# A streaming conformer layer on one core: rows loaded at the fourth gate, taps pinned behind score minima, the channel mean later, a12 moved in odd gates, outputs stored by ScalarE

## The chip, the cores and the metric

One core of a Trainium2 chip runs the whole program. The metric is the time of one execution in microseconds on the device: the kernel before took 3021.13 us in the median of three runs (3019.73 to 3027.58).

Five engines work side by side, each in the order of its own instruction stream: TensorE (PE; its weight loads are listed apart as PEld), VectorE (DVE), ScalarE (ACT), GpSimd (POOL) and SyncE (SP, which here only issues DMAs). An instruction that waits for another engine holds up everything behind it on its own engine. L103 is the line of a helper that records every compute operation, so nearly all compute rows of the profile carry it, and rows are told apart by their tiles.

## What is computed

2048 prompt tokens and 64 sample tokens of width 1024 go through one layer: normalise, one input projection, a convolution branch and a chunk-band attention branch, a gated merge with an output projection, and a gated feed-forward network. Cut to what matters:

```python
h = rms_norm(x, norm1_g) * (1 + sc1) + sh1
glu_a, glu_b, q, k, v, g_conv, g_attn = split(h @ w_in)      # 512 512 512 512 512 1024 1024
u = glu_a * sigmoid(glu_b)
y = depthwise_conv(concat(hist, u), w_dw) + b_dw             # 31 taps, causal, 512 channels
conv_out = silu(layer_norm(y)) @ w_conv_out                  # mean and variance over channels
s = q_h . k_h / 8 + rel_bias; mask to the 64-token chunk and the 8 chunks before it
attn_out = softmax(s) @ v_h @ w_attn_out                     # 8 heads of 64, q and k normed
x = x + gt1 * ((sigmoid(g_conv) * conv_out + sigmoid(g_attn) * attn_out) @ w_o)
gate, up = split((rms_norm(x, norm2_g) * (1 + sc2) + sh2) @ w_ffn_in)   # 2816 each
y_out = x + gt2 * ((silu(gate) * up) @ w_ffn_out)
```

Outputs are y for prompt and sample, and the last convolution inputs, keys and values as states.

## The kernel before

**Number format.** Products of fp32 values are made from high and low halves: an operand is `hi` (rounded, a ScalarE copy) and `lo` (the rest, a subtraction on VectorE or GpSimd), and three matmuls, hi by hi, hi by lo, lo by hi, make one product (`mm3`). In the rows `whi` and `wlo` are halves of weights, `hh` and `hl` of the normalised x, `ph` and `pl` of probabilities.

**Phase 1** runs over four token blocks: 0 to 576 (with the 64 sample tokens), then three of 512. Each block goes through the stages q, 0, k, 1, v, 2, 3, g. The stages q, k and v are projections with rows out. The stages 0 to 3 make u for 128 channels each (`glu`), and start `convolve`: one multiply and thirty multiply-adds on VectorE, one per further tap (rows y<-u,wd,y; 128x606 elements in block 0, else 128x512), into a tile y that has a single buffer. Stage g makes 16 tiles of gates, numbered from 0.

**Work beside the stages** runs in lanes: generators that are pumped between TensorE's products by a planner. The planner adds up estimated load for each engine (`stream.load["pe"]` is its clock, in ns of TensorE) and lets a generator go on when its due time (`yield <time>`) is reached. The order in which this emits instructions is, with a few exceptions, the order on each engine; no times of a real run enter it. The lanes are the norm tiles of the next block, attention heads, the convolution's taps, and the tail.

- *Attention heads.* Block b's heads start after its stage v, so they run beside stages 2, 3 and g and the next block's first stages. A head makes scores tile by tile (rows sc<-kk,q; four matmuls of 128x320 for a full tile) in a PSUM tile with one buffer. VectorE adds the bias and takes the minimum of the negated scores (`softmax_max`; a row named ISA in the order and CUSTOM_DVE_ANT_0 in the trace, pr<-sc,bias), which frees the tile for the next scores; then come exponentials, transposes (ptp) and the product with v (po).
- *Norm tiles* (`norm_tile`). Four tiles of 128 tokens belong to the next block. Each loads its rows x (`load_x`, 512 KB, three buffers, shared with v's stores `vst`), squares on ScalarE, takes the root on GpSimd and VectorE, scales x, makes two groups of four transposes (pt<-ident,x_t), scales them on VectorE, copies hh on ScalarE and subtracts hl on VectorE. The lane is filled at gate 11 (`NORM_G`) and two tiles run at once; a tile that is not done when its first product is due is drained.
- *The tail* (`conv_norm`). When a block's taps are done, GpSimd adds the channels, TensorE makes the mean (pm<-s,ones), VectorE subtracts it, squares are added, a second pm gives the variance, and root, reciprocals, tanh and scales give the branch's silu. At the next block's stage 0 taps and tail are drained.

**Phase 2** runs over three column passes (0 to 576, 576 to 1344, 1344 to 2112). Each merges the two branches with the gates (tg, loaded again from memory), multiplies by w_o, normalises, and runs the feed-forward network over 22 gate tiles f. Gate and up products of a tile are made on 2x2 blocks with seven products instead of eight, named s2, s3, s1, a12, a22, a11 and s4; a product of one half (288 columns in the first pass, 384 in the others) is four times three matmuls. In `up`, s1 accumulates into the PSUM bank that s2 began and that ScalarE has copied to u2 (tile u); a12 has a bank of its own, with a sum and a silu behind it. From f = 5 (`EARLY`) on a12 is made in this way and a11 is made a gate ahead. `up_operands` lists the same order for the producer of the operands; `dn_at` lists the places (`at(n)`) inside an odd gate at which pieces of the down product of a pair are put. The last down product adds into acc, and its rows are stored by SP (L2067) at a due time behind VectorE.

Of the kernel before, what the change touches and what calls it, by code (L numbers as in the profile page):

```python
# [44 lines left out]
TURN_LAG = 2500.0  # L45
KN_LAG = 5000.0
X_LAG = 8000.0
ON_POOL = ()
DMA_LAG = 4000.0
OUT_LAG = 4000.0  # L50
# [2 lines left out]
SIDE_G = 10  # L53
SPLIT_G = 2
NORM_G = 11
NORM_W = 2
SCORE_ROOM = {"dve": 2500}
TURN_NS = 600.0
# [481 lines left out]
def up_operands(f):  # L540

    ops = (["s2", "s3", "s1"] if f else ["s3", "s2", "s1"]) + ["a12"] * (f >= EARLY) + ["a22"] + ["a11"] * (EARLY <= f + 1 < NF) + ["s4"]
    return [(f + (op == "a11"), op) for op in ops]


def dn_at(f):

    return (0, 1, 3, 6 if f == PAIRS[-1] else 4)  # L550


def mod_order():
# [34 lines left out]
def streaming_layer(ctx: ExitStack, tc: tile.TileContext, I, O):  # L588
# [512 lines left out]
    def square(x_t, n):  # L1101
# [4 lines left out]
        dve.tensor_tensor(ssq[:n, 0:1], ssq[:n, 0:1], ssq[:n, 1:2], ALU.add)  # L1106
        return rsqrt_mean(wk, ssq[:n, 0:1], n, 1, D)

    def norm_tile(lo, t, free):

        c = slice(t - lo, t - lo + P)
        x_t = load_x(t, P, wa, "x", 3)
        yield stream.load["pe"] + X_LAG
        r = square(x_t, P)
        yield stream.when("pool")
        dve.tensor_scalar(x_t, x_t, r, None, ALU.mult)
        yield stream.when("dve") + PE_LAG
        for g in range(2):
            pt = ps_g.tile([P, 4, P], F32, tag="gp", name="pt")
            h = temp("h32", (P, 4, P))  # L1120
            for k in range(4):
                pe.transpose(pt[:, k], x_t[:, (4 * g + k) * P : (4 * g + k + 1) * P], ident)
            stream.after("dve", "pe")
            for k in range(4):
                kk = 4 * g + k
                dve.tensor_scalar(h[:, k], pt[:, k], A1[:, kk, 0:1], B1[:, kk, 0:1], ALU.mult, ALU.add)
            yield stream.when("dve")
            yield lambda: free["columns"] >= c.stop
            f = slice(4 * g, 4 * g + 4)
            act.activation(hh[:, f, c], h, AF.Copy)  # L1130
            yield stream.when("act")
            dve.tensor_tensor(hl[:, f, c], h, hh[:, f, c].bitcast(F32), ALU.subtract)
# [66 lines left out]

    now = {"scored": -1, "finished": -1, "bias": None}  # L1200

    def convolve(u, y, ct, b):
        w = UW if b == 0 else HIST + QB
        n = w - HIST
        states = [(cs_s, HIST + SMP)] if b == 0 else [(cs_p, w)] if b == len(PBLOCKS) - 1 else []
        if states:
            yield stream.when("dve") + TURN_LAG
        for rows_, e in states:
            pt = ps_g.tile([P, 512], F32, tag="gp", name="pt")
            pe.transpose(pt[:HIST, :P], u[:, e - HIST : e], ident)  # L1210
            s = wa.tile([HIST, P], F32, tag="cc", name="cc", bufs=2)
            dve.tensor_scalar(s, pt[:HIST, :P], 0.5, None, ALU.mult)
            stream.at(stream.when("dve"), lambda s=s, rows_=rows_: nc.sync.dma_start(rows_[:, ct * P : (ct + 1) * P], s))
            yield
        gps.tensor_copy(hist[:, ct], u[:, w - HIST : w])
        dve.tensor_scalar(y[:, ct, :n], u[:, :n], wd[:, ct, 0:1], bdw[:, ct : ct + 1], ALU.mult, ALU.add)
        for k in range(1, TAPS):
            dve.scalar_tensor_tensor(y[:, ct, :n], u[:, k : k + n], wd[:, ct, k : k + 1], y[:, ct, :n], ALU.mult, ALU.add)
            yield

    def conv_norm(y, c0, n, t0):
        yv = y[:, :, c0 : c0 + n]
        yield lambda: not conv.gens
        s = wk.tile([P, 512], F32, tag="ln_s", bufs=1)

        def total():
# [311 lines left out]
    for b, stage in ORDER:  # L1538
        lo, hi = PBLOCKS[b]
        if stage == "q":  # L1540
            free, ahead = {"columns": 0}, {}
            if b + 1 < len(PBLOCKS):
                ahead = {t: norm_tile(hi, t, free) for t, _ in token_tiles(*PBLOCKS[b + 1])}
        if stage == "q" and b == 0:
            pass
        elif stage in ("q", "k", "v"):
            qkv(b, "qkv".index(stage), norms)
            if stage == "v":

                def heads(b=b):  # L1550
                    work.drain()
                    stream.flush()
                    attention(b)
                    if b == 3:
                        attn.burst, attn.spacing = 2, 0.0

                stream.at(stream.load["pe"] + HEADS_NS, heads)
        elif stage == "g":
            for g in gates(b, free):
                if g == NORM_G:  # L1560
                    for gen in ahead.values():
                        norm_lane.add(gen)
                if g == SIDE_G and b == len(PBLOCKS) - 1:
                    work.drain()
                    conv.drain()
                    stream.flush()
                    side.close()
                    wc = ctx.enter_context(tc.tile_pool(name="wc", bufs=1, side="right"))
                    cs = tile_chunks(*CBLOCKS[0])[0]
                    src = load_mixed(*cs, 0)  # L1570
                    first_gates = gate_columns(*cs, 0)
            norms = ahead
        else:
            if b == 0 and stage == 1:
                bias_rows()
            if stage == 0:
                conv.drain()
                tail.drain()
                y = wk.tile([P, 4, YW], F32, tag="y", name="y")
            conv.add(convolve(glu(b, stage), y, stage, b))  # L1580
            if stage == 3:
                if b == 0:
                    tail.add(conv_norm(y, 0, SMP, 0))
                    tail.add(conv_norm(y, SMP + HIST, QB, SMP))
                else:
                    tail.add(conv_norm(y, 0, QB, lo))
        for _ in range(MODS.get((b, stage), 0)):
            next(mods)
# [158 lines left out]
    for s, (lo, hi) in enumerate(CBLOCKS):  # L1747
# [208 lines left out]
        def rest_of_late(n=99):  # L1956
            while late and n:
                n -= 1
                if next(late[0], None) is None:
                    late.pop(0)  # L1960

        def up(f, ops, at):
# [25 lines left out]
            v = half_piece(1, "v")[:, :half]  # L1988
            keep(v, z)
            rest_of_late()  # L1990
            if f % 2 == 0:
                at(0)
            step(y, "s1", "t1", False, False)
            plus(v, y, v)
            if f % 2:
                at(4)
            if f >= EARLY:
                x = bank("gp")
                step(x, "a12", "b21", True, True)
                plus(x, x, s1)  # L2000
                silu(c1, x)
            if f % 2 == 0:
                at(1)
            step(z, "a22", "t4", False, True)
            plus(z, z, u2)
# [16 lines left out]
        def down(fs, ws):  # L2022

            last = fs[-1] == NF - 1
            for i, (t, n) in enumerate(tiles):
# [19 lines left out]
                for j, ps in enumerate(pss):  # L2045
# [9 lines left out]
                    else:  # L2055
                        if not final:
                            dve.tensor_tensor(ps[:m], ps[:m], both, ALU.add)
                        if n < m:
# [5 lines left out]
                        dve.tensor_tensor(dst, ps[:n], dst if final else x1[j], ALU.add)  # L2064
                        stream.at(
                            stream.when("dve") + OUT_LAG,
                            lambda t=t, n=n, f=f, dst=dst: nc.sync.dma_start(rows(y_p, y_s, t, n)[:, f], dst),  # L2067
                        )
            for _ in fs:
                W.done()  # L2070
# [91 lines left out]
```

## Time and profile before

| | |
|---|---|
| median of three runs | 3021.13 us |
| the profiled execution | 3021.16 us |
| its span, first to last instruction | 3018.7 us |
| mean granted clock of TensorE | 0.987 |
| VectorE, ScalarE, GpSimd busy | 67%, 44%, 32% |
| DMA rate over the span | 229 GB/s |

In rows of the timeline stand the start in us, the duration in us, the engine, line and operation, the tiles out<-in, the shape, the count of merged instructions, and in brackets the idle time ahead of the first and what ended it. A row of waits names what waited and for whom, then total us, number and longest. Matmuls overlap, so their durations add up to more than the time they take. A window's row has for each engine the busy us and the number of instructions, and then the granted clock of TensorE as a share of full speed, the DMA share, and GB/s.

### The profile page before, as it was taken

The page shows a single profiled execution, that of the slowest core. Times are in us where ns is not written, and L with a number is a line of the kernel's source. Part 1 is how long each engine was busy: PE and PEld are TensorE (multiplying, and loading weights), DVE is VectorE, ACT ScalarE, POOL GpSimd, SP SyncE. Part 2 cuts the span into 40 slices and gives each one's busy share as a digit, 9 for nine tenths or more (in the row PEclk, how much of TensorE's full clock was granted, in tenths as well). Part 3 has the DMA queues.
Part 4 walks back from the last instruction along what each step waited for, and adds up shares of the span by engine and source line. Part 5 has one row for each costly group of instructions (what it writes and reads, how often), then busy time and mean ns, then how long its engine had stood idle before and what let it go on. Part 6 is the DMA issues. An engine that isn't in the chain of part 4 may idle for free. (4 is left out here: it accounts for less than half of the span.)

```text
span 3018.7 us, 44690 instructions
## 1 busy us (share of the span) xinstructions
PE 2912.8 (96%) x16199; PEld 2600.1 (86%) x16199; DVE 2019.5 (67%) x3647; ACT 1324.5 (44%) x2375; POOL 956.4 (32%) x599
## 2 busy tenths in 40 slices
PE   7989898999999999999999999999999999999998
PEld 4889776888878788888999989999999898999997
DVE  5896687657966895577766755556565757366567
ACT  3334542563355256464444335434444244333331
POOL 1200120101011101355467323157766331333331
PEclk9999999999999999999999999999999999999999
DMA  9888888887987789886444786446556965355554
GB/s 301 266 279 284 264 293 292 265 255 259 305 273 223 254 284 295 256 295 235 149 146 155 240 286 223 151 141 202 194 170 212 352 206 188 116 168 175 168 163 174
DMA packets 487018, 690.95 MB, mean 229 GB/s; under 512 B 38421, under 2 KB 316809, under 8 KB 486798
## 3 DMA queue, kind: packets, MB, share of 16 engines
q1 hardware_dynamic: 474517, 670.72, 67.8%
q10 hardware_dynamic: 12280, 17.39, 1.6%
q8 instruction: 127, 2.08, 0.3%
q14 instruction: 94, 0.76, 0.1%
HBM read 503.79 MB, written 184.19 MB: 228 GB/s over the span
## 5 line engine op out<-in xcount | busy, mean ns | idle before, releaser
L103 POOL TENSOR_TENSOR wlo<-wst,whi 128x1024 fp32r<-128x1024 f32 (+1 forms) x171 | 388.1, 2274 | 495.3 <-ACT whi L103 448.5
L103 PE MATMUL ps<-t,whi 128*128 128x384 f32 (+1 forms) x2112 | 507.2, 324 | 12.4 <-DVE t L103 5.5
L103 PE MATMUL pd<-whi,hid 128*128 128x512 f32 x1356 | 439.7, 391 | 3.4 <-DVE acc L103 3.4
L103 ACT ACTIVATE whi<-wst 128x1024 fp32r<-128x1024 f32 (+1 forms) x272 | 265.7, 980 | 346.2 <-PE ps L103 117.3
L103 PEld LDWEIGHTS ps<-t,whi 128*128 128x128 f32 x2112 | 371.4, 189 | 21.2 <-DVE t L103 6.4
L103 PE MATMUL ps<-b,whi 128*128 128x384 f32 (+1 forms) x1584 | 379.9, 325 | 1.9 <-DVE pt L103 1.6
L103 DVE SCALAR_TENSOR_TENSOR y<-u,wd,y 128x512 f32<-128x512 f32 (+1 forms) x480 | 369.0, 773 | 8.2
L103 PE MATMUL ps<-hh,whi 128*128 128x512 f32 (+2 forms) x992 | 363.1, 366 | 0.3 <-DVE pl L103 0.3
L103 PE MATMUL ps<-hl,whi 128*128 128x512 f32 (+2 forms) x992 | 345.7, 348 | 0.0
L103 PE MATMUL ps<-hh,wlo 128*128 128x512 f32 (+2 forms) x992 | 345.7, 348 | 0.0
L103 PE MATMUL ps<-t,wlo 128*128 128x384 f32 (+1 forms) x1056 | 341.0, 323 | 0.0
L103 DVE TENSOR_TENSOR acc<-acc,pd 128x512 f32<-128x512 f32 x440 | 289.7, 683 | 69.8 <-PE pd L103 65.9
L103 PEld LDWEIGHTS pd<-whi,hid 128*128 128x128 f32 x1356 | 254.5, 188 | 57.8 <-DVE acc L103 6.5
L103 PEld LDWEIGHTS ps<-b,whi 128*128 128x128 f32 x1584 | 277.0, 189 | 4.9 <-DVE pt L103 2.0
L103 PE MATMUL pd<-wlo,hid 128*128 128x512 f32 x700 | 273.7, 391 | 0.0
L103 PE MATMUL ps<-b,wlo 128*128 128x384 f32 (+1 forms) x792 | 256.3, 324 | 0.0
L103 ACT ACTIVATE pr<-pr,sm 128x640 f32<-128x640 f32 (+3 forms) x272 | 200.0, 747 | 127.6 <-DVE sm L103 125.7
L103 POOL TENSOR_TENSOR r<-t,mhalf 128x1 f32<-128x1 f32 (+3 forms) x68 | 82.3, 1212 | 417.5 <-DVE t L103 373.2
L103 PEld LDWEIGHTS ps<-hh,wlo 128*128 128x128 f32 x992 | 187.4, 189 | 22.7 <-issue 0.4
L103 PEld LDWEIGHTS ps<-hh,whi 128*128 128x128 f32 x992 | 188.0, 190 | 19.3 <-issue 2.7
L103 PEld LDWEIGHTS ps<-hl,whi 128*128 128x128 f32 x992 | 188.2, 190 | 15.5 <-issue 1.7
L103 PEld LDWEIGHTS ps<-t,wlo 128*128 128x128 f32 x1056 | 199.6, 189 | 0.6
(218 smaller groups left out, 5663.0 us busy)
## 6 DMA issues: line engine op xcount, KB each, us to landing
whi<-w_din_h SPq DMA_DIRECT2D x72, 512.0 KB, 4.0
wlo<-w_din_l SPq DMA_DIRECT2D x72, 512.0 KB, 7.3
wst<-sum_d SPq DMA_DIRECT2D x131, 256.0 KB, 2.9
wmod<-in_w_ada SPq DMA_DIRECT2D x48, 512.0 KB, 6.9
sum_d<-ws SPq DMA_DIRECT2D x88, 256.0 KB, 2.2
wst<-in_w_ffn_in SPq DMA_DIRECT2D x85, 256.0 KB, 3.4
wst<-in_w_in SPq DMA_DIRECT2D x40, 512.0 KB, 7.4
wst<-in_w_ffn_in SPq DMA_DIRECT2D x37, 512.0 KB, 5.5
```

Source lines behind the costliest of these rows:

```text
L103: return f(*args, **kw)
```

## The change

Five parts:

1. `ask(t)` loads a norm tile's rows and notes when they should have landed. The first three tiles of the next block are asked for at gate 3 (`ROWS_G`), the fourth when the first tile's second group of transposes is emitted. `norm_tile` then waits for the noted time.
2. `behind(...)`: in blocks 0 and 1 the first tap that is emitted after a score minimum is placed behind that minimum on VectorE.
3. `MEAN_LAG`: the tails of blocks 0, 1 and 2 start 10,000 ns of the planner's clock later.
4. In odd gates from 5 on, a12 with its sum and silu comes ahead of s1, and the last place of the pair's down pieces follows s1.
5. The output rows are issued by ScalarE's queue.

```diff
--- before.py
+++ after.py
@@ -45,6 +45,7 @@
 TURN_LAG = 2500.0
 KN_LAG = 5000.0
 X_LAG = 8000.0
+MEAN_LAG = 10000.0
 ON_POOL = ()
 DMA_LAG = 4000.0
 OUT_LAG = 4000.0
@@ -53,6 +54,7 @@
 SIDE_G = 10
 SPLIT_G = 2
 NORM_G = 11
+ROWS_G = 3
 NORM_W = 2
 SCORE_ROOM = {"dve": 2500}
 TURN_NS = 600.0
@@ -541,13 +543,13 @@
 
 
 
-    ops = (["s2", "s3", "s1"] if f else ["s3", "s2", "s1"]) + ["a12"] * (f >= EARLY) + ["a22"] + ["a11"] * (EARLY <= f + 1 < NF) + ["s4"]
+    ops = (["s2", "s3"] if f else ["s3", "s2"]) + ["a12"] * (f >= EARLY and f % 2) + ["s1"] + ["a12"] * (f >= EARLY and f % 2 == 0) + ["a22"] + ["a11"] * (EARLY <= f + 1 < NF) + ["s4"]
     return [(f + (op == "a11"), op) for op in ops]
 
 
 def dn_at(f):
 
-    return (0, 1, 3, 6 if f == PAIRS[-1] else 4)
+    return (0, 1, 3, 6 if f == PAIRS[-1] else 5)
 
 
 def mod_order():
@@ -1106,11 +1108,19 @@
         dve.tensor_tensor(ssq[:n, 0:1], ssq[:n, 0:1], ssq[:n, 1:2], ALU.add)
         return rsqrt_mean(wk, ssq[:n, 0:1], n, 1, D)
 
+    asked = {}
+
+    def ask(t):
+
+        if t not in asked:
+            asked[t] = load_x(t, P, wa, "x", 3), stream.load["pe"] + X_LAG
+
     def norm_tile(lo, t, free):
 
         c = slice(t - lo, t - lo + P)
-        x_t = load_x(t, P, wa, "x", 3)
-        yield stream.load["pe"] + X_LAG
+        ask(t)
+        x_t, landed = asked.pop(t)
+        yield landed
         r = square(x_t, P)
         yield stream.when("pool")
         dve.tensor_scalar(x_t, x_t, r, None, ALU.mult)
@@ -1120,6 +1130,8 @@
             h = temp("h32", (P, 4, P))
             for k in range(4):
                 pe.transpose(pt[:, k], x_t[:, (4 * g + k) * P : (4 * g + k + 1) * P], ident)
+            if g and t + 3 * P < lo + QB:
+                ask(t + 3 * P)
             stream.after("dve", "pe")
             for k in range(4):
                 kk = 4 * g + k
@@ -1199,6 +1211,10 @@
 
     now = {"scored": -1, "finished": -1, "bias": None}
 
+    def behind(one):
+
+        return tc.issue_after(one.ins) if one is not None else nullcontext()
+
     def convolve(u, y, ct, b):
         w = UW if b == 0 else HIST + QB
         n = w - HIST
@@ -1215,12 +1231,15 @@
         gps.tensor_copy(hist[:, ct], u[:, w - HIST : w])
         dve.tensor_scalar(y[:, ct, :n], u[:, :n], wd[:, ct, 0:1], bdw[:, ct : ct + 1], ALU.mult, ALU.add)
         for k in range(1, TAPS):
-            dve.scalar_tensor_tensor(y[:, ct, :n], u[:, k : k + n], wd[:, ct, k : k + 1], y[:, ct, :n], ALU.mult, ALU.add)
+            with behind(now.pop("least", None) if b < 2 else None):
+                dve.scalar_tensor_tensor(y[:, ct, :n], u[:, k : k + n], wd[:, ct, k : k + 1], y[:, ct, :n], ALU.mult, ALU.add)
             yield
 
     def conv_norm(y, c0, n, t0):
         yv = y[:, :, c0 : c0 + n]
         yield lambda: not conv.gens
+        if t0 < PBLOCKS[-1][0]:
+            yield stream.load["pe"] + MEAN_LAG
         s = wk.tile([P, 512], F32, tag="ln_s", bufs=1)
 
         def total():
@@ -1557,6 +1576,9 @@
                 stream.at(stream.load["pe"] + HEADS_NS, heads)
         elif stage == "g":
             for g in gates(b, free):
+                if g == ROWS_G:
+                    for t in list(ahead)[:3]:
+                        ask(t)
                 if g == NORM_G:
                     for gen in ahead.values():
                         norm_lane.add(gen)
@@ -1988,18 +2010,23 @@
             v = half_piece(1, "v")[:, :half]
             keep(v, z)
             rest_of_late()
+            def factor():
+                if f >= EARLY:
+                    x = bank("gp")
+                    step(x, "a12", "b21", True, True)
+                    plus(x, x, s1)
+                    silu(c1, x)
+
             if f % 2 == 0:
                 at(0)
+            else:
+                factor()
             step(y, "s1", "t1", False, False)
             plus(v, y, v)
             if f % 2:
-                at(4)
-            if f >= EARLY:
-                x = bank("gp")
-                step(x, "a12", "b21", True, True)
-                plus(x, x, s1)
-                silu(c1, x)
-            if f % 2 == 0:
+                at(5)
+            else:
+                factor()
                 at(1)
             step(z, "a22", "t4", False, True)
             plus(z, z, u2)
@@ -2064,7 +2091,7 @@
                         dve.tensor_tensor(dst, ps[:n], dst if final else x1[j], ALU.add)
                         stream.at(
                             stream.when("dve") + OUT_LAG,
-                            lambda t=t, n=n, f=f, dst=dst: nc.sync.dma_start(rows(y_p, y_s, t, n)[:, f], dst),
+                            lambda t=t, n=n, f=f, dst=dst: nc.scalar.dma_start(rows(y_p, y_s, t, n)[:, f], dst),
                         )
             for _ in fs:
                 W.done()
```

What moves, at three places. The first is VectorE at the first head of block 1, with the buffer numbers of the names: u_5234 is the stage's u, y its tap sums, sc_5295 and sc_5310 the head's first two score tiles. Before:

```order
L103 SCALAR_TENSOR_TENSOR u_5234<-tb_5276,ps_5278 128x512
L103 TENSOR_SCALAR y_4293<-u_5234,wd_178,cols_175 128x512
L103 COPY R_5354<-pa_5337 128x256
L103 SCALAR_TENSOR_TENSOR y_4293<-u_5234,wd_178,y_4293 128x512 x4
L103 TENSOR_TENSOR A2_173<-pa_5337,cols_175 128x2x2x2
L103 SCALAR_TENSOR_TENSOR y_4293<-u_5234,wd_178,y_4293 128x512
L103 TENSOR_TENSOR A2_173<-A2_173,cols_175 128x2x2x2
L103 SCALAR_TENSOR_TENSOR y_4293<-u_5234,wd_178,y_4293 128x512 x15
L103 ISA pr_5300,sm_5301<-sc_5295,bias_194 128x640
L103 ISA sm_5301 128x1
L103 SCALAR_TENSOR_TENSOR y_4293<-u_5234,wd_178,y_4293 128x512 x2
L103 ISA pr_5315,sm_5316<-sc_5310,bias_194 128x640
```

After:

```order
L105 SCALAR_TENSOR_TENSOR u_5234<-tb_5276,ps_5278 128x512
L105 TENSOR_SCALAR y_4346<-u_5234,wd_178,cols_175 128x512
L105 COPY R_5354<-pa_5337 128x256
L105 TENSOR_TENSOR A2_173<-pa_5337,cols_175 128x2x2x2
L105 TENSOR_TENSOR A2_173<-A2_173,cols_175 128x2x2x2
L105 ISA pr_5300,sm_5301<-sc_5295,bias_194 128x640
L105 ISA sm_5301 128x1
L105 RECIPROCAL sm_5301<-sm_5301 128x1
L105 ISA pr_5315,sm_5316<-sc_5310,bias_194 128x640
L105 ISA sm_5316 128x1
L105 ISA pr_5332,sm_5333<-sc_5327,bias_194 128x640
```

The twenty taps that stood between u and the first minimum are gone from there, and none stands between the first three minima.

The second is TensorE at the first head of block 3, whose taps are not pinned: sc_10880 to sc_10937 are its four score tiles, and the other rows are a stage's product. Before, from the first score tile to the second and a little further:

```order
L103 MATMUL ps_10866<-hh_195,wlo_10782 128x512
L103 MATMUL sc_10880<-kk_10843,q2_10842 128x320 x4
L103 MATMUL ps_10866<-hh_195,whi_10781 128x512
L103 MATMUL ps_10866<-hl_196,whi_10781 128x512
L103 MATMUL ps_10866<-hh_195,wlo_10782 128x512
L103 MATMUL ps_10866<-hh_195,whi_10781 128x512
L103 MATMUL ps_10866<-hl_196,whi_10781 128x512
L103 MATMUL ps_10866<-hh_195,wlo_10782 128x512
L103 MATMUL sc_10895<-kk_10843,q2_10842 128x320 x4
L103 MATMUL ps_10866<-hh_195,whi_10781 128x512
L103 MATMUL ps_10866<-hl_196,whi_10781 128x512
```

After:

```order
L105 MATMUL ps_10927<-hh_195,whi_10794 128x512
L105 MATMUL ps_10927<-hl_196,whi_10794 128x512
L105 MATMUL ps_10927<-hh_195,wlo_10795 128x512
L105 MATMUL sc_10880<-kk_10843,q2_10842 128x320 x4
L105 MATMUL sc_10895<-kk_10843,q2_10842 128x320 x4
L105 MATMUL sc_10912<-kk_10843,q2_10842 128x320 x4
L105 MATMUL sc_10937<-kk_10843,q2_10842 128x320 x4
L105 MATMUL ptp_10976<-ident_160,pr_10885 128x128
L105 MATMUL ptp_10985<-ident_160,pr_10885 128x128
```

The four score tiles stand one behind the other, where six matmuls of the product stood between each two; on VectorE two taps now stand ahead of the second minimum there, one ahead of the third and of the fourth, and seven ahead of the first.

The third is TensorE at the change from block 0 to block 1, at the block's third norm tile (x_t_3919 before, x_t_2541 after); the products beside it are the last of the tile before it and the first of its own (ps_4117 before). Before:

```order
L103 MATMUL ps_4009<-whi_3931,hl_196 128x512
L103 MATMUL po_4074<-ph_4080,vv_3812 128x512
L103 MATMUL po_4074<-pl_4081,vv_3812 128x512
L103 MATMUL pt_4093<-ident_160,x_t_3919 128x128 x4
L103 MATMUL pt_4105<-ident_160,x_t_3919 128x128 x4
L103 MATMUL sc_4038<-kk_3978,q2_3977 64x320 x2
L103 MATMUL ps_4117<-whi_3430,hh_195 128x512
L103 MATMUL ps_4117<-wlo_3431,hh_195 128x512
```

After:

```order
L105 MATMUL ps_4038<-whi_3444,hh_195 128x512
L105 MATMUL ps_4038<-wlo_3445,hh_195 128x512
L105 MATMUL ps_4038<-whi_3444,hl_196 128x512
L105 MATMUL pt_4046<-ident_160,x_t_2541 128x128 x4
L105 MATMUL ptp_4058<-ident_160,pr_3905 128x128
L105 MATMUL ps_4038<-whi_3681,hh_195 128x512
```

and then, with twelve matmuls between:

```order
L105 MATMUL ps_4038<-whi_3685,hl_196 128x512
L105 MATMUL pt_4091<-ident_160,x_t_2541 128x128 x4
L105 MATMUL po_3995<-ph_4060,vv_3768 128x128
L105 MATMUL po_3995<-pl_4061,vv_3768 128x128
L105 MATMUL pm_4103<-s_4064,ones_165 128x512
L105 MATMUL ps_4038<-whi_3960,hh_195 128x512
```

Before, the eight transposes of the third tile stood together, directly ahead of the tile's own product; now they are in two groups among the products of the tile before.

## Prediction

> **What bounds the kernel now.** The page comes first: busy time by engine, the chain that ended last, and the granted clock.
>
> ```profile
> PE 2912.8 (96%) x16199; PEld 2600.1 (86%) x16199; DVE 2019.5 (67%) x3647; ACT 1324.5 (44%) x2375; POOL 956.4 (32%) x599
> ...
> PE 40%; DMA 2%; DVE 1%; issue 0%; ACT 0%; SPq 0%; DVEq 0%; ACTq 0%
> ```
>
> TensorE is busy for 2912.8 of 3018.7 us, so all its idle time is 105.9 us, and the edit removes no matmul. Whatever it gains comes out of those 105.9 us and out of matmul time lost to a low clock. The view of TensorE's waits splits the idle time:
>
> ```profile
> PE sc L103 <- DVE sm L103: 20.8, 11, 10.1
> PE pt L103 <- DVE x_t L103: 9.4, 6, 3.6
> ...
> PE ps L103 <- ACT hh L103: 5.4, 6, 2.1
> ...
> PE ps L103 <- ACT u L103: 3.3, 6, 0.6
> ```
>
> The columns are total us, times, longest. These four rows, 38.9 us, and the output boundary below are all that the edit's parts aim at. The profiled execution took 3021.16 us, span 3018.7; the median of the three times is 3021.13, so the sum made against 3021.16 needs no correction.
>
> **Pinned taps (blocks 0 and 1).** The timelines of TensorE and VectorE at the first head of block 1:
>
> ```profile
> 493.63 0.80 PE L103 MATMUL sc<-kk,q 128*128 128x320 f32 x4
> ...
> 504.56 1.43 PE L103 MATMUL sc<-kk,q 128*128 128x320 f32 x4 [10.12 <-DVE sm L103]
> 506.92 1.43 PE L103 MATMUL sc<-kk,q 128*128 128x320 f32 x4 [0.93 <-DVE sm L103]
> ...
> 486.34 0.69 DVE L103 SCALAR_TENSOR_TENSOR u<-tb,ps 128x512 f32<-128x512 f32 x1 [9.34 <-PE ps L103]
> ...
> 491.99 11.78 DVE L103 SCALAR_TENSOR_TENSOR y<-u,wd,y 128x512 f32<-128x512 f32 x15
> 503.68 0.82 DVE L103 CUSTOM_DVE_ANT_0 pr<-sc,bias 128x640 f32<-128x640 f32 x1
> ```
>
> The scores stood at 494.43; VectorE, which works in order, reached their minimum at 503.68 because taps stood ahead, and the one score tile held TensorE. In the changed order no tap stands between u and the minimum, so it starts 503.68 - 494.43 = 9.25 us earlier, and the wait falls to 0.87, like the 0.93 of the next tile. The first head of block 0 is alike:
>
> ```profile
> 193.54 0.80 PE L103 MATMUL sc<-kk,q 128*128 128x256 f32 x2 [5.70 <-DVE sm L103]
> ...
> 187.12 6.16 DVE L103 SCALAR_TENSOR_TENSOR y<-u,wd,y 128x606 f32<-128x606 f32 x7
> ```
>
> There 3 taps stay of 7; 4 x 6.16/7 = 3.5 us go, and 2.2 stay. The clock, in windows of 10 us (PE busy, PEld, DVE, ACT, POOL, then the granted clock):
>
> ```profile
> 190.00:200.00 10.00, 5.67 (x19) 4.02 (x20) 8.94 (x21) 3.98 (x12) 0.00 (x0) 0.53 0.27 102
> ...
> 360.00:370.00 10.00, 6.38 (x17) 4.09 (x18) 7.21 (x20) 6.06 (x12) 2.80 (x3) 0.50 1.06 285
> 500.00:510.00 10.00, 3.59 (x11) 2.79 (x12) 8.89 (x17) 3.31 (x7) 0.00 (x0) 0.50 0.45 168
> 510.00:520.00 10.00, 10.00 (x49) 8.11 (x49) 8.31 (x15) 5.98 (x12) 0.53 (x1) 0.83 0.85 191
> ...
> 950.00:960.00 10.00, 7.93 (x37) 6.31 (x36) 7.49 (x22) 4.56 (x9) 3.81 (x3) 0.83 0.24 53
> ```
>
> At clock c, busy time b holds b(1 - c) of loss: 3.59 x 0.50 + 10.00 x 0.17 = 3.5 us at block 1, 5.67 x 0.47 = 2.7 at block 0. With 0.9-us waits left I take all 3.5; with 2.2 left, half of 2.7, 1.3 (ends 0 and 2.7), since 950:960 shows 0.83 after a single 2.07-us wait. The pins save **9.25 + 3.5 + 3.5 + 1.3 = 17.6 us**. The taps themselves are not saved: they run later, under matmuls, while VectorE still has a third of the span free.
>
> *A rule beside this.* The Trainium skill, "TensorE: Matmul & The Clock Gate", "What's actually happening", says that the clock halves after an idle window of about 3.4 us. The trace agrees at the 10.12-us wait and not at 2.07 us, which also lost clock; by the rule alone block 0 would regain all 2.7 us and the time be 1.4 us shorter.
>
> **What the displaced taps cost.** Order decides this, not the amount of work. Blocks 2 and 3 have no pins. In block 3's first head the four score tiles now stand back to back; before, six matmuls lay between each:
>
> ```profile
> 1061.18 0.74 PE L103 MATMUL sc<-kk,q 128*128 128x320 f32 x4
> ...
> 1063.15 0.74 PE L103 MATMUL sc<-kk,q 128*128 128x320 f32 x4
> ```
>
> They were 1.97 us apart and waited for nothing. Back to back, each of three waits costs about 0.93 as at 506.92, and two taps (0.785 each by 11.78/15) stand ahead of the second minimum, one ahead of the third and fourth: (0.93 + 0.95) + 2 x 1.1 = **4.0 us** lost, between 2.8 (no tap hurts) and 8 (the seven taps ahead of the first minimum are late too, or the clock drops). Block 2's first head now has two score tiles adjacent and eight taps ahead: **1.5** (0.9 to 5). Later heads and norm tiles that meet deferred taps: no row has them; between 0 and 6, and I take **2.5**, three waits like 0.93.
>
> **Rows earlier.** Each block's tiles waited for x, loaded only as the norm began. SP's and TensorE's rows at the change from block 0 to 1:
>
> ```profile
> 353.57 0.42 SPq L1098 DMA_DIRECT2D x_t<-in_x_prompt  x1
> ...
> 362.40 0.63 ACT L103 ACTIVATE junk<-x_t 128x512 f32<-128x512 f32 x1 [3.52 <-DMA x_t<-in_x_prompt]
> ...
> 326.55 0.63 PE L103 MATMUL pt<-ident,x_t 128*128 128x128 f32 x4 [1.57 <-DVE x_t L103]
> ...
> 360.74 1.97 PE L103 MATMUL pt<-ident,x_t 128*128 128x128 f32 x8 [3.64 <-DVE x_t L103]
> ...
> 366.36 0.80 PE L103 MATMUL ps<-whi,hh 128*128 128x512 f32 x1 [2.14 <-ACT hh L103]
> ...
> 378.03 0.50 PE L103 MATMUL ps<-whi,hh 128*128 128x512 f32 x1 [1.06 <-ACT hh L103]
> ```
>
> Three tiles are now asked for at gate 3, eight gates before the norms begin, the fourth when the first tile's buffer is free; the third tile's two transpose groups stand 20 rows apart among products, 10 rows ahead of the product that reads them. The first row gives 1.57. The next three are 6.84; I leave 2.0 for the chain x, square, root, transposes, scale, and take 4.8 (ends 3 and 6.8). The window 360:370 returns 6.38 x 0.50 = 3.2. At the change from block 1 to 2:
>
> ```profile
> 667.22 1.09 PE L103 MATMUL pt<-ident,x_t 128*128 128x128 f32 x8 [0.55 <-DVE x_t L103]
> ...
> 670.03 0.50 PE L103 MATMUL ps<-whi,hh 128*128 128x512 f32 x1 [1.14 <-ACT hh L103]
> ```
>
> Of this 1.7 I take 1.5. Together **11.1 us**. The eight issues are the same ones, about 0.45 us each on SP, moved past loads that are prefetched; the three buffers, shared with v's stores, are held some 30 us longer, and a store that waits for one delays only VectorE's copies out of PSUM, about 1 us, inside the 2.5 above.
>
> **The later mean.** 10 us later frees VectorE and the TensorE slots at the norm tiles, but the tail of block 0 (sum, root, reciprocals, silu) must end before block 1's first tap, since y has one buffer. I cost it at 0, between -1 and +4.
>
> **Odd gates.** In the first column pass each of six odd gates has one wait:
>
> ```profile
> 1506.46 0.53 PE L103 MATMUL ps<-t,whi 128*128 128x288 f32 x2 [0.57 <-ACT u L103]
> ...
> 1684.97 0.53 PE L103 MATMUL ps<-t,whi 128*128 128x288 f32 x2 [0.55 <-ACT u L103]
> ```
>
> s1 adds on into the PSUM bank that ScalarE must first copy out as u, and only the product s3 lies between; with a12 there as well, one product more covers a wait that is a third of a product (rival 2 prices one at 2.1 us for 384 columns, three quarters of that at 288). I take all **3.3** (ends 0 and 3.3). In the passes of 384 columns there is nothing to gain, and I cost the new order at 0 because nothing waits there:
>
> ```profile
> 1950.00:2025.00 75.00, 75.00 (x399) 70.77 (x398) 39.86 (x70) 26.38 (x44) 36.71 (x19) 1.00 0.48 158
> ```
>
> Some 24 low-half subtractions move from GpSimd to VectorE, 0.68 us each, spread over 1,600 us in which VectorE is half idle: 0.
>
> **Output stores.** SP issues ten in a row ahead of two gate loads, which the first merge of the next pass awaits:
>
> ```profile
> 1744.64 7.42 SPq L2067 DMA_DIRECT2D out<-acc  x10
> 1752.15 1.79 SPq L1085 DMA_DIRECT2D tg<-g_d  x2
> ...
> 1757.80 0.59 PE L103 MATMUL ps<-cin,whi 128*128 128x384 f32 x2 [1.55 <-DVE t L103]
> 1762.64 0.59 PE L103 MATMUL ps<-cin,whi 128*128 128x384 f32 x2 [0.24 <-DVE t L103]
> 1766.33 0.62 PE L103 MATMUL ps<-cin,whi 128*128 128x384 f32 x2 [1.24 <-DVE m L103]
> ...
> 1737.29 1.06 ACT L103 ACTIVATE whi<-wup 128x1024 fp32r<-128x1024 f32 x1 [17.88 <-PE pd L103]
> ```
>
> ScalarE has nothing for 17.88 us there, so the issues fit, and tg goes out 7.4 us earlier than its first use needs by 1.55: **3.0 us** saved, between 0 and 3.0. At the second boundary and the end no wait hangs on them.
>
> *A rule against it.* The Trainium skill, "DMA: Bandwidth & Descriptors", "Issuing engines are not separate DMA queues", says that issues from another engine share the same DMA engines and save only issue time. Here the issue time is 7.42 us, longer than the wait; were the shared transfers the limit, the sum would be 3.0 us longer.
>
> **Sum.** 17.6 + 11.1 + 3.3 + 3.0 = 35.0 us saved, 4.0 + 1.5 + 2.5 = 8.0 spent, net 27: 3021.16 - 27.0 = **2994 us**.
>
> **Rivals.**
> 1. *The waits move with the taps.* The deferred taps stand ahead of later minima and the tail of block 0 is late: 8.0 spent becomes 8 (block 3) + 5 (block 2) + 6 + 4 (mean) = 23. Then 3021 - 35 + 23 = 3009 us. For it: VectorE is 83 to 89% busy from 500 to 520, where the taps must go. Against: nothing but the next u and the tail needs them.
> 2. *Slower: a12 comes before its weights.* It now starts one product earlier: 12 matmuls, about 2.1 us at 0.53 for three. The nine odd gates from 5 on, in three passes, are 27 places; whole lateness costs 57 us, and the time is 2994 + 57 = 3051. It decides at (27 + 9)/27 = 1.3 us of lateness per gate, where 3030 is passed. For it: some halves are now made on VectorE, behind other work. Against: 75.00 busy of 75 us; weights are ready ahead.
> 3. *The parts do less than they say.* Minima wait for something else, x for its queue: only half the heads' and rows' gain comes, 14 instead of 28.7, with all 8 spent: 3021 - 14 - 6 + 8 = 3009; without the 6 us of the two last parts, 3015.
>
> **How the numbers follow.** Forecast 0.58 (2983 to 3004: all residual waits gone and no new ones, or each cost at its upper half); rival 1 0.17 (to 3011); rival 3 0.15, half of it at or above 3012; rival 2 0.07; a mishap of some us short of that 0.03. A measurement of this kernel tells 0.3% from no change, 9 us: below 3012.1 is faster, above 3030.2 slower. Faster: 0.58 + 0.16 + 0.07 = 0.81; slower 0.07; same 0.12. The range 2981 to 3013 leaves out rival 2, part of 3 and a little below.
>
> **What would show it.** Right: the rows sc <- sm fall from 20.8 to some 14 us in total, with the longest about 2.2 and new ones near block 3's first head; x_t and hh together from 14.8 to about 5; no row <- u; tg issued before the last stores; the clock near 1 at block 1's first head. Wrong: a new wait of 5 us or more on sm or x_t at the block changes, any wait of TensorE in the 384-column passes at odd gates, or a <- part row at the end of block 0's tail.

## Result and profile after

| | before | after |
|---|---|---|
| median | 3021.89 us (15 runs) | 3010.99 us (15 runs) |
| the profiled execution, its span | 3021.16, 3018.7 us | 3008.78, 3006.7 us |

The ratio is 0.9965, 95% interval 0.9956 to 0.9974: 10.6 us faster, between 8 and 13. The prediction was 27 us, 2994 us. The sign was right and the time lies inside the range, but the gain is less than half of the one forecast. What follows looks for the other 16 us.

The page of the changed kernel, busy time by engine, and its view of TensorE's waits (total us, times, longest):

```profile
PE 2918.5 (97%) x16199; PEld 2601.2 (87%) x16199; DVE 2031.4 (68%) x3671; ACT 1322.3 (44%) x2375; POOL 914.3 (30%) x575
...
PE sc L105 <- DVE sm L105: 15.0, 13, 2.8
PE ptp L105 <- ACT pr L105: 7.8, 9, 2.1
...
PE ps L105 <- DVE m L105: 2.5, 3, 1.2
...
PE ps L105 <- DVE hl L105: 1.9, 2, 1.7
PE pt L105 <- DVE x_t L105: 1.9, 2, 1.4
```

TensorE's idle time fell by 17.7 us (105.9 to 88.2). Its busy time grew by 5.7 with the same number of matmuls, so some of them ran longer. The rows that the change aimed at did fall: x_t from 9.4 to 1.9, u from 3.3 to nothing. But waits on minima only fell from 20.8 to 15.0, those on pr (exponentials) grew from 2.1 to 7.8 and on m (a merge tile) from 1.2 to 2.5, and hl is new. TensorE's timeline shows where:

```profile
188.24 0.41 PE L105 MATMUL sc<-kk,q 128*128 128x128 f32 x2 [2.41 <-DMA kk<-k_d]
189.68 0.79 PE L105 MATMUL sc<-kk,q 128*128 128x256 f32 x2 [1.03 <-DVE sm L105]
...
269.10 0.39 PE L105 MATMUL ptp<-ident,pr 64*128 64x64 f32 x3 [2.09 <-ACT pr L105]
301.36 0.39 PE L105 MATMUL ptp<-ident,pr 64*128 64x64 f32 x3 [1.55 <-ACT pr L105]
365.18 0.50 PE L105 MATMUL ps<-whi,hl 128*128 128x512 f32 x1 [1.70 <-DVE hl L105]
...
398.70 0.73 PE L105 MATMUL sc<-kk,q 128*128 128x512 f32 x2 [2.79 <-DVE sm L105]
...
502.13 1.10 PE L105 MATMUL sc<-kk,q 128*128 128x320 f32 x4 [1.29 <-DVE sm L105]
...
1057.26 0.85 PE L105 MATMUL sc<-kk,q 128*128 128x320 f32 x4 [1.34 <-DVE sm L105]
...
1751.22 0.62 PE L105 MATMUL ps<-cin,whi 128*128 128x384 f32 x2 [0.44 <-DVE m L105]
...
2376.57 0.62 PE L105 MATMUL ps<-cin,whi 128*128 128x384 f32 x2 [0.85 <-DVE m L105]
2380.16 0.62 PE L105 MATMUL ps<-cin,whi 128*128 128x384 f32 x2 [1.21 <-DVE m L105]
```

The two big waits ahead of first minima, 5.70 and 10.12, are now 1.03 and 1.29; the three near 360 became 1.70. In their place stand a chain of 1 to 3 us waits at the change from block 0 to block 1 (365 to 440), and two at the second output boundary, where there was none.

Gate issues on ScalarE's queue serve as milestones that all kernels pass. The 13th of block 0 and the first of block 1, before and after:

```profile
262.50 0.33 ACTq L1289 DMA_DIRECT2D g_d<-gate  x1
...
533.12 0.33 ACTq L1289 DMA_DIRECT2D g_d<-gate  x1
```

```profile
260.39 0.34 ACTq L1308 DMA_DIRECT2D g_d<-gate  x1
...
528.78 0.33 ACTq L1308 DMA_DIRECT2D g_d<-gate  x1
```

From one to the other it took 270.6 us before and 268.4 after. In this stretch the forecast had put 12.75 us from the pins and 9.6 from the rows, and 2.2 came. The last gate (1224.16 before, 1215.10 after) shows phase 1 at 9.1 us gained of 20.7 forecast, and phase 2 at 2.9 of 6.3.

### The profile page after: what moved, and what is told of

Its sections match the earlier page's. It is cut to its first block, busy times and chain, and to the rows that moved or that the text cites. A ratio compares the mean times of both kernels' runs of the same rounds, so it can differ in the third digit from the quotient of the medians.

```text
span 3006.7 us, 44645 instructions
## 1 busy us (share of the span) xinstructions
PE 2918.5 (97%) x16199; PEld 2601.2 (87%) x16199; DVE 2031.4 (68%) x3671; ACT 1322.3 (44%) x2375; POOL 914.3 (30%) x575
## 4 chain that ended last, share of the span: by engine, by line
PE 81%; DVE 8%; DMA 6%; issue 2%; ACT 1%; POOL 1%; SPq 1%; ACTq 0%; DVEq 0%; POOLq 0%
PE ps L105 52%; PE pd L105 14%; PE pw L105 6%; DVE y L105 3%; PE po L105 2%; PE sc L105 2%; PE ptp L105 2%; DVE wlo L105 1%; PE pt L105 1%; DMA kk<-k_d 1%; PE pa L105 1%; POOL r L105 1%; DMA cin<-o_d 1%; DMA tg<-g_d 1%; DVE pr L105 1%
```

## Experiments

Every ratio is to the kernel before on the same chip, five rounds each; 0.001 is 3 us. Parts are numbered as in the section on the change.

**1. Without the lag (part 3).**

```diff
-        if t0 < PBLOCKS[-1][0]:
-            yield stream.load["pe"] + MEAN_LAG
```

> The change without its third part: the tails of blocks 0 to 2 start as before, without the 10 us. What is to be explained: phase 1 gained 9 us where 21 were forecast, and new waits of TensorE stand from 340 to 445 us (minima 2.79, 1.35, 1.32, 0.89; exponentials 1.55, 0.98; hl 1.70). Theory A (the later mean crowds VectorE and ScalarE at block 1's start): those waits go, 5 to 8 us come back, the time is about 3004. Theory B (pinned taps run later and stand in the way there): the waits stay, the time is within 2 us of 3011. Theory C (the later mean was what emptied the norm tiles' way): waits of x_t or hh come back near 360 us and the time is 3013 to 3016.

Ratio 0.9941 (0.9926 to 0.9956), against 0.9965 with the lag: theory A. The minima waits between 340 and 445 fall to one of 0.70, and all idle time there from 12.1 to 4.7 us. But one wait is new, in TensorE's timeline:

```profile
298.27 0.69 PE L105 MATMUL pm<-s,ones 128*128 128x64 f32 x2 [7.32 <-POOL s L105]
```

So the lag has a use, at the tail of the 64 sample rows, and a price elsewhere. The two intervals just touch; experiments 5 and 9 separate them.

**2 to 4. Without the pins, without the rows, without parts 4 and 5.** The edits put back the lines of the kernel before: no tap is pinned; no `ask` at gate 3 or in the transposes; a12 behind s1, stores on SP.

> The change without its second part: no tap is pinned behind a minimum. By the forecast the waits of about 10 us at block 1's first head and about 5 us at block 0's come back with their half clock: some 17 us longer, 3028. Theory B (the pinned taps are paid for later): the waits of 262 to 282 us and 340 to 445 us, about 10 us together with the low clock at 270, go, so that the net is 3 to 8 us longer, 3014 to 3019. Theory A: nothing goes, about 3026.

> The change without its first part: x rows are loaded when the norm tile starts, as before. By the forecast 11 us longer, 3022, with waits on x_t of 3 us or more and hh of 2 us at 360 and a half clock there. If the rows only changed places with other waits (the waits of 262 to 282 and 365 to 380 go in turn), 3011 to 3014.

> The change with odd gates and the output stores as before. By the forecast 6.3 us longer, 3017: six waits of 0.55 on u in the first pass and 3.0 us at 1750 come back; the waits on m at 2376 and 2380 (0.85 and 1.21) go if the stores on ScalarE's queue made them, and then it is 4 us longer, 3015.

Ratios 0.9976 (0.9965 to 0.9987), 0.9951 (0.9938 to 0.9965) and 0.9967 (0.9954 to 0.9980). Taking the pins away costs 3 us, with intervals of 3 us on both sides. That is the size that theory B gave, but its waits did not go (2.09 at 272 and 2.78 at 404 are still there), while 4.79 and 7.47 came back at the two first heads; why the medians differ by so little stays open. Taking the rows away does not lengthen the kernel at all, though its trace has 4.60 on x_t at 361 and a clock of 0.67 from 360 to 370 again. This contradicts the forecast's 11 us: in the presence of the lag the rows bring nothing. Parts 4 and 5 together are worth less than can be seen here, with 6.3 forecast.

**5. The lag for the sample tail alone.**

```diff
-        if t0 < PBLOCKS[-1][0]:
+        if t0 == 0:
```

> The change, with the 10 us of lag kept for the sample rows' tail of block 0 alone; the other tails start as before. Without any lag the kernel took 0.9941 of before, and one wait of 7.32 us stood at 298 for the sample tail's sums. Theory A (the lag pays at the sample tail and costs 7 us and more where it puts block 0's prompt tail among block 1's first heads): the 7.32 goes, the waits from 340 to 445 stay away (idle there about 5 us instead of 12), some 4 to 7 us below the kernel without lag: ratio 0.992. If the lag has no such place (the difference of the first experiment was chance), ratio 0.9965 as for the whole change.

Ratio 0.9932 (0.9920 to 0.9944): theory A. Its interval does not meet that of the whole change, and 10 us lie between the two, give or take 5. The wait of 7.32 is gone from its trace (pm stands at 302.98 without one), and so are the minima waits from 340 to 445; but 3.72 on kk at 416 and 2.06 on pr at 419 stand there, and all idle time there is 7.3 us where 5 was expected. Whether that also gains time over no lag at all (0.9941) the intervals leave open.

**6 to 8. Each part alone on the kernel before:** pins; rows; a12 and stores.

> The kernel before with the pins alone. Forecast: 17.6 saved less at most 4 for later heads, ratio 0.9955 to 0.994. Theory B (pinned taps are paid for later): the two first heads gain 11 to 13 us of idle time in the trace and other minima of blocks 0 and 1 give 6 to 9 of it back, ratio 0.998 to 0.999.

> The kernel before with the early rows alone. Forecast: 11.1 saved, less 4.0 at block 3's first head: ratio 0.9975. If the rows only change places with other waits: x_t and hh waits fall from 14.8 to under 5 us in the trace, but ratio 0.999 to 1.001, with block 3's first head (1055 to 1060) losing 3.5 to 4 us and the rest lost at the change from block 0 to 1.

> The kernel before with a12 moved and the stores on ScalarE's queue alone. Forecast: 6.3 saved, ratio 0.998. If the stores give back at the second boundary what they gain at the first: the six waits on u go (3.3 us), 1757 to 1766 falls from 3.0 to below 1, and waits of 2 us or more on m appear near 2385: about 3 us saved, ratio 0.999.

Ratios 0.9969 (0.9958 to 0.9980), 0.9971 (0.9961 to 0.9981) and 0.9989 (0.9979 to 0.9999): 9.4, 8.8 and 3.3 us. They add up to 21 us, and the change without the lag has 18, which is the same within the intervals. So the three parts add up without the lag; with it they do not (experiment 3). For the pins neither expectation held; 9.4 is between. For a12 and the stores the second did: all six waits on u are gone, and 2.97 and 1.32 on m stand at 2393 and 2397. Their own cost shows in GpSimd's and TensorE's timelines, pins alone:

```profile
293.61 0.29 POOL L105 TENSOR_TENSOR s<-s,y 128x64 f32<-128x64 f32 x1 [52.23 <-DVE y L105]
...
293.96 0.69 PE L105 MATMUL pm<-s,ones 128*128 128x64 f32 x2 [5.55 <-POOL s L105]
```

VectorE runs block 0's last taps until 293.5. TensorE comes to the mean's matmul at 288.4 and stops until the sums are made. No kernel without pins has this wait at the sample tail. The rows alone came in above their forecast net of 7.1.

**9. The lag for block 0's prompt tail alone.**

```diff
-        if t0 < PBLOCKS[-1][0]:
+        if t0 == SMP:
```

> The change with the 10 us of lag kept for block 0's prompt tail alone. Theory A: this one lag costs what the lag cost as a whole, and the sample tail's wait for GpSimd's sums (7.32 at 298 without lag) is back too: against the kernel without any lag (0.9941) about 9 us longer, ratio 0.997, with minima waits of 1.3 to 2.8 us from 365 to 440. If the lag of blocks 1 and 2 was what cost, the ratio is that of no lag, 0.994.

Ratio 0.9978 (0.9968 to 0.9987): theory A again, 11 us above the kernel without lag, and the 7.32 on pm is back at 300 as in that kernel. This one tail's lag carries the whole price. The milestones agree: from the 13th gate issue of block 0 to the first of block 1 it takes 268.4 and 266.4 us with the whole lag (the change and experiment 4, whose phase 1 is the same), 275.5 here, but 261.1 without lag and 261.1 and 259.2 with the sample tail's alone (experiments 5 and 12). Behind that stretch, where the tails of blocks 1 and 2 run, no loss of the whole lag shows: 686.3 us to the last gate, against 685.7 in experiment 5. Where the price is paid, TensorE's, VectorE's and GpSimd's timelines show:

```profile
394.57 0.33 PE L105 MATMUL sc<-kk,q 128*128 128x128 f32 x2
402.90 0.80 PE L105 MATMUL sc<-kk,q 128*128 128x256 f32 x2 [7.03 <-DVE sm L105]
...
386.45 3.39 DVE L105 RECIPROCAL s<-s 128x128 f32<-128x128 f32 x4 [1.78 <-ACT s L105]
...
396.25 0.69 DVE L105 TENSOR_TENSOR kn<-kn,r 128x512 f32<-128x512 f32 x1 [5.15 <-POOL r L105]
396.86 0.54 DVE L105 TENSOR_SCALAR y<-y,cols 128x512 f32<-128x512 f32 x1
...
402.54 0.29 DVE L105 CUSTOM_DVE_ANT_0 pr<-sc,bias 128x128 f32<-128x128 f32 x1
...
389.99 4.64 POOL L105 TENSOR_TENSOR y<-y,s 128x512 f32<-128x512 f32 x4 [6.83 <-DVE s L105]
394.59 1.63 POOL L105 TENSOR_TENSOR r<-t,mhalf 128x8 f32<-128x8 f32 x1
```

Read from the end: TensorE waits 7.03 us for the minimum at 402.54, whose scores stood at 394.9. VectorE comes to it late because kn, the next block's keys, waited 5.15 us for their root r, and because ten operations of the tail follow kn ahead of the minimum. GpSimd's root is late because the tail's four multiplies, 4.64 us, stand ahead of it. Behind the wait the clock is 0.55 from 400 to 410, where experiment 1 has 1.00. The whole change has the same pattern, with GpSimd's y<-y,s at 381.80 (4.82 us) ahead of r at 386.58, kn waiting 3.82 and a minimum 2.79; some taps stand ahead of that minimum as well. In experiments 1 and 5 no kn near there waits longer for r than 1.82 us.

The late root costs time where a minimum stands behind it. Experiment 3, with the whole lag and late rows, has kn waiting 3.91 at 396, but VectorE's next minimum comes at 414, TensorE waits for none, and the stretch between the milestones takes 263.1 us (262.2 with the pins alone). So with late rows the whole lag costs nothing that shows, and with early rows some 10 us.

**10. Pins and the sample tail's lag on the kernel before.**

> The kernel before with the pins, and the lag for the sample tail alone. The pins alone had a wait of 5.55 us on pm<-s at 294, with a half clock behind it, which no other kernel without pins has: pinned taps finish the sample's last channels later. Theory: the lag takes that wait away, and 5 to 8 us with it: ratio 0.9969 becomes 0.995. If the wait only moves (to transposes of the sample heads or to another sum), 0.9965 to 0.997.

Ratio 1.0004 (0.9994 to 1.0014): a miss. The wait on pm at 294 is gone as expected, but with rows loaded late two others grew, and a half clock came with them (0.50 from 360 to 370):

```profile
361.37 1.97 PE L105 MATMUL pt<-ident,x_t 128*128 128x128 f32 x8 [5.67 <-DVE x_t L105]
...
367.62 0.80 PE L105 MATMUL ps<-whi,hh 128*128 128x512 f32 x1 [4.29 <-ACT hh L105]
```

The sample tail and the prompt tail share a lane and follow each other, so a lag on the first moves the second too. The pattern of experiment 9 is there again: kn waits 3.71 at 394, and minima behind it 2.20. Experiment 3, which has late rows and this lag too, is 16 us shorter; which of its other parts does that was not tried. What a lag is worth depends on what it is moved into.

**11. Of the first three rows only the third early, with the sample tail's lag.**

```diff
-                    for t in list(ahead)[:3]:
+                    for t in list(ahead)[2:3]:
```

> As the lag for the sample tail alone (0.9932), but only the third tile's rows are asked for at gate 3; the first two tiles load as the norm begins, as before the change. Theory: early rows of the first two tiles let their norms start at gate 11 at once, which moves TensorE's fill work from behind the sample heads' exponentials (waits of 2.09 and 1.55 on ptp at 268 and 299, half clock there): those go, 3 to 6 us less, ratio 0.9915. If the first two tiles' rows are worth their 1.57 us and no more hangs on them, 0.9935.

Ratio 0.9956 (0.9941 to 0.9971), 7 us longer than 0.9932, though the intervals just touch: a miss. The wait of 2.09 on transposes near 268 went, as expected, but that of 1.55 stayed (1.85 at 298), and 1.35 on x_t, 1.78 on pm and 3.37 on a minimum came between 326 and 392. The last is the pattern of experiment 9 once more, with kn waiting 4.80 for its root ahead of it. The first two tiles' early rows are worth more than the wait on them.

**12. Stores on ScalarE's queue in the first column pass alone, with the sample tail's lag.**

```diff
-  lambda t=t, n=n, f=f, dst=dst: nc.scalar.dma_start(
+  lambda t=t, n=n, f=f, dst=dst, lo=lo: (nc.sync if lo else nc.scalar).dma_start(
```

> As the lag for the sample tail alone (0.9932), with stores on ScalarE's queue for the first column pass only, on SP's for the others. Theory: the waits on m near 2373 and 2377 (1.86 and 1.38), which all kernels with the stores on ScalarE's queue show and none of the others, go: 2 to 3 us less, ratio 0.9925. If the waits come from something else, they stay, and the ratio is 0.9932.

Ratio 0.9912 (0.9899 to 0.9924), median 2998.71 us: the fastest of all, by the ratio 26.6 us below before. The waits on m are gone. ScalarE's timeline at the second boundary shows the difference, the whole change first:

```profile
2348.36 12.17 ACTq L2094 DMA_DIRECT2D out<-acc  x8
2361.54 1.06 ACT L105 ACTIVATE whi<-wup 128x1024 fp32r<-128x1024 f32 x1 [16.92 <-PE pd L105]
...
2372.68 1.06 ACT L105 ACTIVATE whi<-wst 128x1024 fp32r<-128x1024 f32 x1 [10.09 <-DMA wst<-in_w_attn_out]
...
2375.46 0.47 ACT L105 ACTIVATE m<-ps 128x384 fp32r<-128x384 f32 x1
```

and with the stores of this pass on SP again:

```profile
2353.43 1.06 ACT L105 ACTIVATE whi<-wup 128x1024 fp32r<-128x1024 f32 x1 [16.91 <-PE pd L105]
2358.49 1.06 ACT L105 ACTIVATE whi<-wst 128x1024 fp32r<-128x1024 f32 x1 [4.00 <-DMA wst<-in_w_attn_out]
...
2361.17 0.47 ACT L105 ACTIVATE m<-ps 128x384 fp32r<-128x384 f32 x1
```

The first merge of the pass stands in TensorE's order at 2362.74 after and at 2354.64 here (rows ps<-cin, with 0.55 and 0.57 us of wait on acc). Against it, the first copy, whi<-wup, runs 1.2 us ahead in both; the next, whi<-wst, 9.9 us behind instead of 3.9, and m 12.7 instead of 6.5. That copy waits for its load: SP issues the loads of wst from 2362.19 on, while with the stores on SP they go out from 2345.64 on. What SP itself waited for in the whole change from 2345 to 2372 says why (L1095 loads cin, L383 loads wst):

```profile
SPq L1095 <- DMA out<-acc: 6.1, 2, 3.5
SPq L383 <- DMA cin<-c_d: 5.6, 2, 3.3
SPq L383 <- DMA cin<-o_d: 2.9, 1, 2.9
```

The loads of cin wait until two of the stores have landed; ScalarE issues these one by one as their acc is ready, eight of them in 12.17 us. The loads of wst stand behind the loads of cin on SP and wait for those in turn. In experiment 12 SP waits for no store there. All eight kernels with these stores on ScalarE's queue have this wait of SP (3.8 to 7.5 us) and waits of 2.1 to 4.3 us on m, and none of the six with them on SP's has either. Why a load of cin is made to wait for a store the traces do not show. The trace of experiment 5 accounts for 3.2 us (1.86 and 1.38); that the two kernels differ by 6 is within their intervals. The edit puts the last pass's stores back on SP too; from the last matmul to the end it is 8.0 us in the whole change and here.

## Why the prediction was wrong, step by step

- **The later mean, "I cost it at 0, between -1 and +4".** This is the step that failed. Measured: about 10 us lost (experiment 5 against the whole change), and 11 by experiment 9, outside the range given. The prediction looked at the tail's end, which y's single buffer forces before block 1's first tap, and not at what stands behind the tail's operations on GpSimd and VectorE: the roots of the next block's keys and the current heads' minima. Experiment 9 shows them in line. The sum also let parts add that do not: with late rows the same lag costs nothing that shows (experiment 3). Rival 1, "The waits move with the taps", priced the mean with 4, and its 3009 us lies near the time measured, but by other terms (8 at block 3's first head and 5 at block 2's, where 3.7 and 1.1 came).
- **Output stores, "At the second boundary and the end no wait hangs on them".** Wrong at the second boundary: some 3 us by the trace of experiment 5, and 2.06 in the changed kernel's. The first boundary's 3.0 became 0.44 in the profile after, but between 0.5 and 2.2 in the other kernels with these stores there, and it was 1.6 to 3.0 without them: the gain there was about 1 us, and more was given back. The prediction showed ScalarE idle for 17.88 us and asked whether the issues fit; it did not ask which loads on SP wait until these stores have landed. With the stores moved in the first pass alone this loss goes.
- **Pins, 17.6 us.** The idle part was right at both places: 5.70 became 1.03 and 10.12 became 1.29 (forecast 2.2 and 0.87). The clock part was mis-sized: 4.8 us was to come back, but the windows at both heads (first and last row) are still at 0.56 and 0.66, and a new one at 0.66 stands behind the wait of 2.09 at 269 (middle row):

```profile
190.00:200.00 10.00, 9.06 (x36) 7.19 (x36) 5.61 (x16) 5.57 (x15) 0.00 (x0) 0.56 0.41 142
270.00:280.00 10.00, 10.00 (x55) 9.87 (x54) 6.92 (x14) 3.26 (x7) 0.00 (x0) 0.66 0.94 308
500.00:510.00 10.00, 7.77 (x27) 6.31 (x28) 4.13 (x12) 4.83 (x9) 0.00 (x0) 0.66 1.07 369
```

  By the sum used in the prediction the first lost 2.7 us of matmul time before and 9.06 x 0.44 = 4.0 after, and the third 3.5 before (with the window behind it) and 7.77 x 0.34 = 2.6 after. A run of waits of 0.5 to 2.4 us did to the clock what one of 5.70 had done. At block 0's first head this is so in all ten kernels with pins (0.55 to 0.70 from 190 to 200); at block 1's it varies, and experiments 1 and 12 have 1.00 from 490 to 520. The Trainium skill, "TensorE: Matmul & The Clock Gate", "What's actually happening", ties the drop to an idle window of about 3.4 us; no single wait near these windows reaches that, so by waits of that length alone no drop was due here, and the measured windows decide.
- **What the displaced taps cost, 8.0 us.** Block 3's first head was as forecast: 1.47 + 1.34 + 0.92 = 3.7 us where 4.0 was taken, but it came with the rows (they alone show 0.93 three times, the kernels without early rows nothing), since these change what lies between the scores. At block 2's first head 1.1 us came where 1.5 was taken. The 2.5 for later heads was too small for the pins alone, whose trace has 5.55 on pm and a clock of 0.66 from 290 to 300; the lag on the sample tail takes that wait away.
- **Rows, 11.1 us.** Right in total, but not in place. Rows alone brought 8.8 net of block 3's head (forecast 7.1), and the waits on x_t and hh fell from 14.8 to 2.5 us in the changed kernel. But between the milestones, where 9.6 was forecast, the rows bring 1 to 2 us: 268.2 with rows alone against 270.6 before and 269.2 in experiment 8 (the same phase 1 as before), and 261.1 with rows and pins against 262.2 with pins. From the first gate of block 1 to the last gate the eight kernels with all rows early take 685.7 to 691.5 us and the five with late rows 691.0 to 696.2, on average 6 us more, where the forecast had no net gain. So the size was in part luck; where those 6 us come from was not traced.
- **Odd gates, 3.3 us.** Right: all six waits on u are gone (from 1500 to 1730 TensorE is now busy for 230.00 of 230 us, 226.68 before).

So each wait that the change aimed at went or fell to about 1 us. The change carries two losses of its own, the prompt tail's lag and the stores of the second pass, and without these two it reaches 26.6 us, near the 27.0 forecast. That agreement is partly luck, since not all of the clock came back, the rows gained little where they were to, and the blocks after the second gained more than forecast (the wait of 2.73 on kk at 855 went, and that of 2.07 at 953). Shown by runs are the two losses; that the other three parts add up holds without the lag and within the intervals. Not tried: the lag on blocks 1 and 2 by itself, and a tail whose multiplies stand behind the root on GpSimd.

## What to carry to other kernels

When work is moved later to make room, list what stands behind it at its new place on every in-order engine that it uses, the slow ones too, and who waits for that: here four multiplies on GpSimd delayed a root, the root a VectorE operation, and that the minimum for which TensorE stopped. When DMA issues move to another engine, ask not only whether that engine has idle time but when the data will be ready, and which loads wait until the transfer has landed: here eight stores took 12.17 us of ScalarE's queue to issue, and loads on SP waited for them. Parts of a change that each gain can lose together: measure each alone and the whole without each.

## What the hardware did that was not expected

The same wait does not always lower the clock. The kernel of experiment 4 has the same instructions in the same order in phase 1 as the whole change and the same wait of 2.09 us near 268, but its window there ran at full clock (0.66 in the whole change):

```profile
270.00:280.00 10.00, 10.00 (x74) 9.81 (x74) 9.61 (x19) 5.04 (x12) 0.00 (x0) 1.00 0.98 335
```

74 matmuls instead of 55 started in it, and its last gate came at 1211.61 instead of 1215.10. Two more pairs with the same phase 1 differ alike at the last gate: 1224.16 before and 1228.28 in experiment 8, 1206.57 and 1203.45 in experiments 5 and 12. So one profile of this kernel is good to some 3 to 4 us in phase 1, and the first wait for keys in block 0, 1.36 us in the profile before, was between 1.62 and 3.79 in the twelve experiments' profiles.
